# State space products in 64x64 quarters of the array, one per group

## The chip, the cores and the metric

One core of a Trainium2 chip runs the whole kernel. The metric is the device time of one execution in microseconds. TensorE multiplies (a stationary block of up to 128x128 weights is loaded, a moving operand streams past it, results go to PSUM), VectorE and ScalarE do the elementwise work, GpSimd sets constants up, and most transfers are issued from SyncE's queue.

## The reference

A hybrid decoder layer over 16 meta tokens and 256 tokens of width 2048, all in float32:

```
h = RMSNorm(x);  q|k|v|u = h @ W_in
a = sliding-window attention(q, k, v)         16 heads, 4 kv heads, window 128, ALiBi, sinks
s = GLU(S5(u))
x += concat(RMSNorm(a), RMSNorm(s)) @ W_out
x += relu(RMSNorm(x) @ W_up)^2 @ W_down       8192 wide
```

The part that the change touches is S5, a diagonal state space model: 64 groups of 16 channels, each of which drives a complex state of 64 entries.

```
lam_bar = exp(lam * delta);  b_bar = ((lam_bar - 1) / lam) * b
state[t] = lam_bar * state[t-1] + b_bar @ u[t]
y[t] = Re(c @ state[t]) + d * u[t];  g = gelu(y);  s = g * sigmoid(g @ W_glu + b_glu)
```

## The kernel before

Large products split float32 operands into a high and a low part (hi, lo) and take three products of these; weights arrive in units of 512 KB, and `part` has ScalarE write hi and VectorE write lo, up to four units ahead of their use. The phases follow each other on TensorE: u0, k, v, q0, u1, q1, u2, u3 (projections), then wt (the attention half of W_out), g (GLU), wb (the other half of W_out), and the MLP (up, dn). Attention and the state space model are side work, generators that `step` feeds between the units. A planner keeps a clock for VectorE, ScalarE and TensorE, adds a price to it for each instruction (`product` prices TensorE), and feeds side work as long as the two vector clocks run less than `lead` ahead of TensorE's. A scheduler of the language then orders each engine's instructions by a simulation, with priorities. Each engine and SyncE's queue execute in order.

The state space model works in chunks of CT = 4 tokens: 68 chunks (4 of meta tokens, 64 of tokens). Groups are taken in 32 pairs (the pair's two groups fill 128 rows: 2 x 64 states), and the pairs in four sets Q of 8. For each Q:

- `prod` (L621) builds a table of 8 x 4 x 16 entries per state row from the powers of lam_bar (Fr, Fi, Ar, Ai) and b or c: three VectorE operations into a temporary, then two ScalarE copies that spread the two groups into a table of 8 x 4 x 2 x 16, so that each group sits beside zeros.
- `ssm_in` (L639) builds Vr, Vi; `ssm_vt` (L652) transposes them, 16 transposes of 128x128 and four copies from PSUM.
- `ssm_out` (L672) builds Wr, Wn; takes kp, the response of a chunk to itself, with products of 128x32 weights; spreads it with a mask (gm) into the first 32 rows of MT, adds the diagonal d on VectorE, and copies shifted blocks of it to the other rows with three transfers inside SBUF.
- `ssm_states` (L739): z = VT x U, two products of 128x128 by 68 for each pair, then VectorE rotates them; `ssm_scan` (L771) runs the recurrence on VectorE.
- `ssm_y` (L805): y = MT x U + Wr x Xr + Wn x Xi, three products of 128x128 by 64 for each pair; Gelu on ScalarE; a transfer to DRAM (dg) and four back into gT, whose rows are channels.

U is u in rows of (token in the chunk, group, channel); `u_out` (L705) writes it to DRAM and reads it back with four transfers. Every 128x128 block of VT, Wr, Wn and MT is block diagonal over the pair's two groups: half of it is zeros.

```
q = slice(64 * hf, 64 * hf + 64)
nc.tensor.matmul(sp[:, 0:144], lhsT=self.qT[q, m, 0:P], rhs=self.KT[q, j, 0:144], start=True, stop=True)
```

These two lines of `score` (L956) are the one place of before where products of half the rows alternate: heads lie in rows 0-63 and 64-127, and each head writes a PSUM tile of its own.

`late` is a one that ScalarE makes when attention is done; what is scaled with it can't run earlier, so that Gelu's table is loaded once Exp is over.

Of the kernel before, what the change touches and what calls it, by code (L numbers as in the profile page):

```python
# [29 lines left out]
CT = 4  # L30
# [34 lines left out]

class Paced:
# [19 lines left out]
class PacedCore:  # L86
# [8 lines left out]
    def product(self, out, kw):  # L95
        n = math.prod(out.shape[1:])
        return 0.11 * PRICE[2] if "rhs" not in kw else n / 2400 if kw["rhs"].dtype == F32R else PRICE[2] * max(n, math.prod(kw["lhsT"].shape[1:])) / 600
# [5 lines left out]
class Trunk:  # L103
# [232 lines left out]
    def constants(self):  # L336
        nc, c = self.nc, self.cst

        w = self.st.tile([P, D // 2], F32, tag="xn", bufs=4, name="zeros")[:, 0:256]
# [149 lines left out]
    def ssm_params(self):  # L489
# [48 lines left out]
        pw = lambda nm, n: sp.tile([P, n, NPAIR], F32, name=nm)  # L538
# [82 lines left out]
    def prod(self, Q, z, xr, xi, yr, yi, op):  # L621

        tt = self.tt
        js = slice(8 * Q, 8 * Q + 8)
        vb = lambda a: a[:, js, :].unsqueeze(2).to_broadcast([P, 8, CT, 16])
        fb = lambda a: a[:, :, js].rearrange("p s j -> p j s").unsqueeze(3).to_broadcast([P, 8, CT, 16])
        t5 = self.spb.tile([P, 8, CT + 1, 16], F32, tag="gt0", bufs=2, name=f"gt0_{Q}")
        t0, t1 = t5[:, :, 1:, :], self.spb.tile([P, 8, CT, 16], F32, tag="gt1", name=f"gt1_{Q}")
        tt(t0, vb(xr), fb(yr), MULT)
        tt(t1, vb(xi), fb(yi), MULT)  # L630
        yield
        tt(t0, t0, t1, op)
# [4 lines left out]
        return t5  # L637

    def ssm_in(self, Q):  # L639
# [4 lines left out]
        if Q == 0:  # L644
            nc.vector.tensor_reduce(out=self.gm, in_=self.m8.rearrange("p (k x) -> p x k", x=2), axis=AX.X, op=ADD)
            nc.vector.tensor_reduce(out=self.blk2, in_=self.m8.rearrange("p (x k) -> p x k", x=2), axis=AX.X, op=ADD)
        Vr, Vi = self.ops[0:2]
        (br, bi) = self.B
        yield from self.prod(Q, Vr, br, bi, self.Fr, self.Fi, SUB)
        yield from self.prod(Q, Vi, br, bi, self.Fi, self.Fr, ADD)  # L650

    def ssm_vt(self, Q):  # L652
        nc = self.nc
        VT = []
        Vr, Vi = self.ops[0:2]
        for nm, V in (("r", Vr), ("i", Vi)):
            vt = self.spb.tile([P, 8, P], F32, tag=f"VT{nm}", name=f"VT{nm}{Q}")
            v2 = V.rearrange("p j s g h -> p j (s g h)")
            for n0 in (0, 4):
                tp = self.ps(f"!vt{nm}{Q}_{n0}").rearrange("p (n c) -> p n c", c=P)  # L660
                for n in range(4):
                    nc.tensor.transpose(out=tp[:, n, :], in_=v2[:, n0 + n, :], identity=self.ident)
                nc.scalar.activation(vt[:, n0:n0 + 4, :], tp, AF.Copy)
                yield
            VT.append(vt)
# [6 lines left out]
    def ssm_out(self, Q):  # L672
# [4 lines left out]
        Vr, Vi, Wr, Wn = self.ops  # L677
        MT = self.MT
        cr, nci = self.C
        Wc = []  # L680
        for W, c, a in ((Wr, cr, (self.Ar, self.Ai)), (Wn, nci, (self.nAi, self.Ar))):
            t = yield from self.prod(Q, W, cr, nci, *a, ADD)
            nc.scalar.activation(t[:, :, 0, :], c[:, js, :], AF.Copy)
            Wc.append(t)

        kp = self.ps(f"!kp{Q}")[0:32, :].rearrange("p (j h) -> p j h", h=64)
        for n in range(8):
            for k, (V, w) in enumerate(zip((Vr, Vi), Wc)):
                nc.tensor.matmul(kp[:, n, :], lhsT=V[:, n, 3, :, :].rearrange("p g h -> p (g h)"),
                                 rhs=w[:, n, 0:CT, :].rearrange("p k h -> p (k h)"), start=k == 0, stop=k == 1)  # L690
            if n % 4 == 3:
                yield
        q = slice(0, 32)
        for g in range(2):
            nc.scalar.activation(MT[q].rearrange("p j (k g h) -> p (j k) g h", g=2, h=16)[:, :, g, :],
                                 kp.rearrange("p j (k h) -> p (j k) h", h=16), AF.Copy, scale=self.gm[q, g:g + 1])
        dI = self.spb.tile([P, 8, CT, 16], F32, tag="gt1", name=f"dI{Q}").rearrange("p j s h -> p (j s h)")[:, 0:256].rearrange("p (j h) -> p j h", h=32)
        tt(dI[q], self.ident[q, q].unsqueeze(1).to_broadcast([32, 8, 32]), self.dd[q, js].unsqueeze(2).to_broadcast([32, 8, 32]), MULT)
        tt(MT[q, :, 0:32], MT[q, :, 0:32], dI[q], ADD)
        yield  # L700
        for t in range(1, CT):
            nc.sync.dma_start(out=MT[32 * t:32 * t + 32, :, 32 * t:], in_=MT[q, :, 0:P - 32 * t])
        yield

    def u_out(self, mp, acc):  # L705
# [10 lines left out]
        def back():  # L716
            for s in range(CT):
                self.nc.sync.dma_start(out=self.U[32 * s:32 * s + 32, 8 * mp:8 * mp + 8, :].rearrange("r (q m) c -> r q (m c)", q=4),
                                       in_=dr[:, s, :, :].rearrange("(q r) m c -> r q (m c)", q=4))
# [19 lines left out]
    def ssm_states(self, Q):  # L739
# [65 lines left out]
    def ssm_y(self, Q):  # L805
        nc, X, MT, (Wr, Wn) = self.nc, self.X, self.MT, self.ops[2:4]
# [254 lines left out]
    def attn_end(self):  # L1061
# [291 lines left out]
```

## Time and profile before

| what | value |
|---|---|
| median of 3 runs | 1052.19 us (1051.99 to 1052.55) |
| profiled execution, its own time | 1052.78 us |
| its span | 1051.0 us |
| granted TensorE clock | 0.999 |
| TensorE, VectorE, ScalarE busy | 99%, 64%, 49% |
| HBM read, written | 186.03 MB, 4.26 MB |
| state space work lies between | 30 and 275 us of the span |

PE is TensorE, PEld its weight loads, DVE VectorE, ACT ScalarE, POOL GpSimd, SPq SyncE's queue. In a group of instructions stand line, engine, operation, output <- inputs, shapes and count, then busy us and mean ns of one, then idle time of the engine before them and what ended it. A matmul's end is modelled, and ends of neighbours overlap: what one costs is read from the distance of starts, or from the pieces of the chain of waits. The functions of the planner hand instructions on, so most rows carry a helper's line (L80, L81); go by the names of the tiles.

### The profile page before, as it was taken

To read this page: it belongs to the slowest core of one execution; us is meant where nothing else is said; L and a number is where in the kernel's file an instruction comes from. 1 tells how busy PE (TensorE), PEld (TensorE's weight loads), DVE (VectorE), ACT (ScalarE), POOL (GpSimd) and SP (SyncE) were. 2 spreads that over 40 slices of the span, in tenths; PEclk is the share of its full clock that TensorE was granted. 3 is DMA by queue.
4 is the path that set the end of the run, shared out by engine and by line. 5 is a ranking of instruction groups with operands and counts; after the bars stand their busy time and mean duration, and the time that the engine had idled before them with its cause. 6 is when DMAs were issued, how large, how long until landed. Compare 5 with 4: busy or idle time off the path is not lost.

```text
span 1051.0 us, 14959 instructions
## 1 busy us (share of the span) xinstructions
PE 1043.7 (99%) x5732; PEld 897.5 (85%) x5732; DVE 670.5 (64%) x1108; ACT 518.4 (49%) x744; POOL 10.1 (1%) x62
## 2 busy tenths in 40 slices
PE   8999999999999999999999999999999999999998
PEld 7989788888988888888888888888888888888886
DVE  8998877758677766555466655556565545665553
ACT  5845767563656544433445443344453344544332
POOL 3000000000000000000000000000000000000000
PEclk9999999999999999999999999999999999999999
DMA  9663424345556666566666656566656666665763
GB/s 323 219 201 103 141 90 149 104 148 179 166 177 196 184 191 190 186 194 197 193 190 185 196 185 197 193 189 196 187 185 194 198 189 194 184 195 184 216 216 105
DMA packets 145994, 192.07 MB, mean 183 GB/s; under 512 B 9697, under 2 KB 97889, under 8 KB 145537
## 3 DMA queue, kind: packets, MB, share of 16 engines
q1 hardware_dynamic: 145360, 190.54, 58.0%
q8 instruction: 45, 0.74, 0.3%
q10 hardware_dynamic: 560, 0.56, 0.2%
q14 instruction: 29, 0.23, 0.1%
HBM read 186.03 MB, written 4.26 MB: 181 GB/s over the span
## 4 chain that ended last, share of the span: by engine, by line
PE 98%; DMA 1%; ACT 0%; SPq 0%; issue 0%; DVE 0%; ACTq 0%
PE up L81 34%; PE dn L81 33%; PE u L81 5%; PE q L81 4%; PE wt L81 4%; PE wb L81 4%; PE y L80 2%; PE g L81 2%; PE pv L80 2%; PE k L81 1%; PE z L80 1%; PE v L81 1%; PE s L80 1%; PE kp L80 1%; DMA xT<-in_xT 1%; PE pt L80 1%
## 5 line engine op out<-in xcount | busy, mean ns | idle before, releaser
L80 DVE TENSOR_TENSOR lo<-raw,hi 128x1024 fp32r<-128x1024 f32 x328 | 401.1, 1223 | 284.6 <-ACT hi L80 284.2
L80 ACT ACTIVATE hi<-raw 128x1024 fp32r<-128x1024 f32 x328 | 347.3, 1060 | 363.7 <-PE dn L81 195.5
L81 PE MATMUL up<-h,hi 128*128 128x512 f32 x1024 | 245.6, 391 | 0.0
L81 PEld LDWEIGHTS up<-h,hi 128*128 128x128 f32 x1024 | 188.1, 188 | 36.2
L81 PE MATMUL dn<-hi,ah 128*128 128x512 f32 x512 | 199.2, 389 | 0.0
L81 PE MATMUL dn<-lo,ah 128*128 128x512 f32 x512 | 199.2, 389 | 0.0
L81 PE MATMUL dn<-hi,al 128*128 128x512 f32 x512 | 199.2, 389 | 0.0
L81 PEld LDWEIGHTS up<-h,lo 128*128 128x128 f32 x1024 | 131.5, 191 | 5.1
L81 PE MATMUL up<-h,lo 128*128 128x256 f32 x1024 | 133.1, 283 | 0.0
L81 PEld LDWEIGHTS dn<-hi,ah 128*128 128x128 f32 x512 | 96.1, 188 | 20.0
L81 PEld LDWEIGHTS dn<-hi,al 128*128 128x128 f32 x512 | 96.1, 188 | 20.0
L81 PEld LDWEIGHTS dn<-lo,ah 128*128 128x128 f32 x512 | 96.1, 188 | 19.8
L81 ACT ACTIVATE r<-up 128x256 f32<-128x256 f32 x64 | 24.0, 375 | 56.3 <-PE up L81 56.3
L81 DVE TENSOR_TENSOR r<-up,r 128x256 f32<-128x256 f32 x64 | 26.9, 421 | 29.0 <-ACT r L81 29.0
L81 PE MATMUL wt<-hi,ma 128*128 128x512 f32 x128 | 41.0, 399 | 0.0
L81 PE MATMUL u<-hTl,hi 128*128 128x272 f32 x96 | 28.9, 301 | 0.0
L81 PE MATMUL u<-hTh,lo 128*128 128x272 f32 x96 | 28.6, 298 | 0.0
L81 PEld LDWEIGHTS wt<-hi,ma 128*128 128x128 f32 x128 | 23.7, 188 | 5.3
L81 PE MATMUL u<-hTh,hi 128*128 128x272 f32 x96 | 28.3, 295 | 0.0
L81 ACT ACTIVATE ah<-s 128x512 fp32r<-128x512 f32 x32 | 20.2, 632 | 16.0 <-DVE s L81 16.0
L81 DVE SCALAR_TENSOR_TENSOR xm<-dn,rs_h,xm 128x512 f32<-128x512 f32 x32 | 22.5, 743 | 7.8 <-PE dn L81 7.8
L81 PE MATMUL q<-lo,hTh 128*128 128x512 f32 x64 | 25.8, 404 | 0.0
(292 smaller groups left out, 1154.8 us busy)
## 6 DMA issues: line engine op xcount, KB each, us to landing
raw<-in_w_up SPq DMA_DIRECT2D x128, 512.0 KB, 3.9
raw<-in_w_down SPq DMA_DIRECT2D x128, 512.0 KB, 3.8
raw<-in_w_in SPq DMA_DIRECT2D x39, 512.0 KB, 4.3
raw<-in_w_out SPq DMA_DIRECT2D x32, 512.0 KB, 4.1
raw<-in_w_glu SPq DMA_DIRECT2D x8, 512.0 KB, 4.3
x<-in_x SPq DMA_DIRECT2D x4, 512.0 KB, 8.4
xm<-in_x SPq DMA_DIRECT2D x2, 1024.0 KB, 7.7
out<-xm SPq DMA_DIRECT2D x8, 256.0 KB, 5.1
```

The source lines that it names most:

```text
L80: return f(*args, **kw)
L81: return f(*args, **kw)
```

## The change

The two groups of a pair are no longer one 128x128 product with zeros, but two of 64x64: rows and columns 0-63 for one, 64-127 for the other, into the same PSUM tile. The tables lose their zeros, and a row of a table is ordered (channel, token in the chunk). The powers lie as (pair, power). V and W are written by VectorE straight into the tables. V is turned by products with the identity in place of transposes. kp reads a small copy V3, which alone keeps the zeros, and a W shifted by one power, wc. MT is laid out in `km` on 32 partitions, one copy for each token of the chunk, with the diagonal written by ScalarE, and goes through DRAM into 128 rows. U and gT come back in one transfer each. The planner's price of such a product is halved, and the buffers for rows of x are six.

```
-        return ... else PRICE[2] * max(n, math.prod(kw["lhsT"].shape[1:])) / 600
+        return ... else PRICE[2] * max(n, math.prod(kw["lhsT"].shape[1:])) * kw["lhsT"].shape[0] / P / 600
...
-        self.ops = [self.spb.tile([P, 8, CT, 2, 16], F32, name=nm) for nm in ("Vr", "Vi", "Wr", "Wn")]
-        self.MT = self.spb.tile([P, 8, P], F32, name="MT")
-        nc.vector.memset(self.ops[0], 0.0)
-        for z in self.ops[1:] + [self.MT]:
-            g.memset(z, 0.0)
+        self.km = self.spb.tile([P, CT * 513], F32, name="km")[0:32, :]
+        self.V3 = self.spb.tile([P, 2, 8, 2, 16], F32, name="V3")
+        nc.vector.memset(self.km, 0.0)
+        g.memset(self.V3, 0.0)
...
-        t = self.st.tile([P, D // 2], F32, tag="xn", bufs=4, name=f"x{k}{h}")[0:src.shape[0], :]
+        t = self.st.tile([P, D // 2], F32, tag="xn", bufs=6, name=f"x{k}{h}")[0:src.shape[0], :]
...
-        pw = lambda nm, n: sp.tile([P, n, NPAIR], F32, name=nm)
+        pw = lambda nm, n: sp.tile([P, NPAIR, n], F32, name=nm).rearrange("p j s -> p s j")
...
-        vb = lambda a: a[:, js, :].unsqueeze(2).to_broadcast([P, 8, CT, 16])
-        fb = lambda a: a[:, :, js].rearrange("p s j -> p j s").unsqueeze(3).to_broadcast([P, 8, CT, 16])
-        t5 = self.spb.tile([P, 8, CT + 1, 16], F32, tag="gt0", bufs=2, name=f"gt0_{Q}")
-        t0, t1 = t5[:, :, 1:, :], self.spb.tile([P, 8, CT, 16], F32, tag="gt1", name=f"gt1_{Q}")
-        tt(t0, vb(xr), fb(yr), MULT)
+        vb = lambda a: a[:, js, :].unsqueeze(3).to_broadcast([P, 8, 16, CT])
+        fb = lambda a: a[:, :, js].rearrange("p s j -> p j s").unsqueeze(2).to_broadcast([P, 8, 16, CT])
+        t1 = self.spb.tile([P, 8, 16, CT], F32, tag="gt1", name=f"gt1_{Q}")
+        tt(z, vb(xr), fb(yr), MULT)
         tt(t1, vb(xi), fb(yi), MULT)
         yield
-        tt(t0, t0, t1, op)
-        for g in range(2):
-            q = slice(64 * g, 64 * g + 64)
-            self.nc.scalar.activation(z[q, :, :, g, :], t0[q], AF.Copy, scale=1.0 if self.late is None else self.late[q, :])
+        tt(z, z, t1, op)
...
-            for n0 in (0, 4):
-                tp = self.ps(f"!vt{nm}{Q}_{n0}").rearrange("p (n c) -> p n c", c=P)
-                for n in range(4):
-                    nc.tensor.transpose(out=tp[:, n, :], in_=v2[:, n0 + n, :], identity=self.ident)
-                nc.scalar.activation(vt[:, n0:n0 + 4, :], tp, AF.Copy)
+            tp = self.ps(f"!vt{nm}{Q}").rearrange("p (n c) -> p n c", c=64)
+            for n in range(8):
+                for q in GROUPS:
+                    nc.tensor.matmul(tp[q, n, :], lhsT=V[q, n, :, :].rearrange("p h s -> p (h s)"), rhs=self.ident[q, q], start=True, stop=True)
+            nc.scalar.activation(vt, tp, AF.Copy)
...
+            nc.scalar.activation(w[:, :, :, 0], c[:, js, :], AF.Copy)
+            nc.scalar.activation(w[:, :, :, 1:], W[:, :, :, 0:CT - 1], AF.Copy)
...
+        for k, V in enumerate(self.ops):
+            for g, q in enumerate(GROUPS):
+                nc.scalar.activation(self.V3[q, k, :, g, :], V[q, :, :, 3], AF.Copy)
...
-        for t in range(1, CT):
-            nc.sync.dma_start(out=MT[32 * t:32 * t + 32, :, 32 * t:], in_=MT[q, :, 0:P - 32 * t])
+        for s in range(CT - 1):
+            o = one if self.late is None else self.late[0:32, :]
+            nc.scalar.activation(km[:, s, :, :, s + 1:], kp[:, :, :, 1:CT - s], AF.Copy, scale=o)
+        tt(dI, kp[:, :, :, 0], dI, ADD)
+        same = self.km.rearrange("p (s x) -> p s x", x=513)[:, :, 0:512].rearrange("p s (y k) -> p s y k", k=CT)[:, :, :, 0]
+        nc.scalar.activation(same, dI.rearrange("p j h -> p (j h)").unsqueeze(1).to_broadcast([32, CT, 128]), AF.Copy, ...)
+        dk = self.dram.tile([32, CT * 512], F32, name=f"dk{Q}")
+        nc.sync.dma_start(out=dk, in_=self.km[:, 0:CT * 512])
+        self.MT = self.spb.tile([P, 8, 64], F32, tag="MT", name=f"MT{Q}")
+        nc.sync.dma_start(out=self.MT.rearrange("p j x -> p (j x)"), in_=dk.rearrange("r (s x) -> (r s) x", s=CT))
...
-                    nc.tensor.matmul(z[k][:, n, :], lhsT=VT[k][:, 4 * o + n, :], rhs=self.U[:, j0 + 4 * o + n, :], start=True, stop=True)
+                    for q in GROUPS:
+                        nc.tensor.matmul(z[k][q, n, :], lhsT=VT[k][q, 4 * o + n, :], rhs=self.U[q, j0 + 4 * o + n, :], start=True, stop=True)
...
-            nc.tensor.matmul(yp[:, n, :], lhsT=MT[:, n, :], rhs=self.U[:, 8 * Q + n, MCH:NCH], start=True, stop=False)
-            for k, W in enumerate((Wr, Wn)):
-                nc.tensor.matmul(yp[:, n, :], lhsT=W[:, n, :, :, :].rearrange("p s g h -> p (s g h)"), rhs=X[k][:, n, MCH - 1:NCH - 1], start=False, stop=k == 1)
+            for q in GROUPS:
+                nc.tensor.matmul(yp[q, n, :], lhsT=MT[q, n, :], rhs=self.U[q, 8 * Q + n, MCH:NCH], start=True, stop=False)
+            for k, W in enumerate(self.W):
+                for q in GROUPS:
+                    nc.tensor.matmul(yp[q, n, :], lhsT=W[q, n, :, :].rearrange("p h s -> p (h s)"), rhs=X[k][q, n, MCH - 1:NCH - 1], start=False, stop=k == 1)
```

Here `GROUPS = (slice(0, 64), slice(64, 128))`.

More of the change, by code (lines that the diff above doesn't have):

```diff
@@ L63 @@
 FAR = -1e32
+GROUPS = (slice(0, 64), slice(64, 128))
 class Paced:
@@ L96, in product @@
         n = math.prod(out.shape[1:])
-        return 0.11 * PRICE[2] if "rhs" not in kw else n / 2400 if kw["rhs"].dtype == F32R else PRICE[2] * max(n, math.prod(kw["lhsT"].shape[1:])) / 600
+        return 0.11 * PRICE[2] if "rhs" not in kw else n / 2400 if kw["rhs"].dtype == F32R else PRICE[2] * max(n, math.prod(kw["lhsT"].shape[1:])) * kw["lhsT"].shape[0] / P / 600
     def __getattr__(self, name):
@@ L337, in constants @@
         nc, c = self.nc, self.cst
-        w = self.st.tile([P, D // 2], F32, tag="xn", bufs=4, name="zeros")[:, 0:256]
+        w = self.st.tile([P, D // 2], F32, tag="xn", bufs=6, name="zeros")[:, 0:256]
         nc.vector.memset(w, 0.0)
@@ L643, in ssm_in @@
             nc.gpsimd.tensor_scalar(self.C[1], self.C[1], -1.0, None, op0=MULT)
-        if Q == 0:
-            nc.vector.tensor_reduce(out=self.gm, in_=self.m8.rearrange("p (k x) -> p x k", x=2), axis=AX.X, op=ADD)
             nc.vector.tensor_reduce(out=self.blk2, in_=self.m8.rearrange("p (x k) -> p x k", x=2), axis=AX.X, op=ADD)
-        Vr, Vi = self.ops[0:2]
+            self.i16 = self.cst.tile([32, 16], F32, name="i16")
+            self.tt(self.i16, self.ident[0:32, 0:16], self.ident[0:32, 16:32], ADD)
         (br, bi) = self.B
-        yield from self.prod(Q, Vr, br, bi, self.Fr, self.Fi, SUB)
-        yield from self.prod(Q, Vi, br, bi, self.Fi, self.Fr, ADD)
+        self.ops = [self.spb.tile([P, 8, 16, CT], F32, tag=nm, name=f"{nm}{Q}") for nm in ("Vr", "Vi")]
+        yield from self.prod(Q, self.ops[0], br, bi, self.Fr, self.Fi, SUB)
+        yield from self.prod(Q, self.ops[1], br, bi, self.Fi, self.Fr, ADD)
     def ssm_vt(self, Q):
@@ L654, in ssm_vt @@
         VT = []
[L655 to L658, printed above, removed]
-            for n0 in (0, 4):
-                tp = self.ps(f"!vt{nm}{Q}_{n0}").rearrange("p (n c) -> p n c", c=P)
-                for n in range(4):
-                    nc.tensor.transpose(out=tp[:, n, :], in_=v2[:, n0 + n, :], identity=self.ident)
-                nc.scalar.activation(vt[:, n0:n0 + 4, :], tp, AF.Copy)
-                yield
+        for nm, V in zip("ri", self.ops):
+            vt = self.spb.tile([P, 8, 64], F32, tag=f"VT{nm}", name=f"VT{nm}{Q}")
+            tp = self.ps(f"!vt{nm}{Q}").rearrange("p (n c) -> p n c", c=64)
+            for n in range(8):
+                for q in GROUPS:
+                    nc.tensor.matmul(tp[q, n, :], lhsT=V[q, n, :, :].rearrange("p h s -> p (h s)"), rhs=self.ident[q, q], start=True, stop=True)
+                if n == 3:
+                    yield
+            nc.scalar.activation(vt, tp, AF.Copy)
+            yield
             VT.append(vt)
@@ L676, in ssm_out @@
         js = slice(j0, j0 + 8)
-        Vr, Vi, Wr, Wn = self.ops
-        MT = self.MT
+        one = 1.0 if self.late is None else self.late
         cr, nci = self.C
[L680 to L686, printed above, removed]
+        self.W, Wc = [], []
@@ new lines, in ssm_out @@
+        for nm, c, a in (("Wr", cr, (self.Ar, self.Ai)), ("Wn", nci, (self.nAi, self.Ar))):
+            W, w = (self.spb.tile([P, 8, 16, CT], F32, tag=m, name=f"{m}{Q}") for m in (nm, nm + "c"))
+            yield from self.prod(Q, W, cr, nci, *a, ADD)
+            nc.scalar.activation(w[:, :, :, 0], c[:, js, :], AF.Copy)
+            nc.scalar.activation(w[:, :, :, 1:], W[:, :, :, 0:CT - 1], AF.Copy)
+            self.W.append(W)
+            Wc.append(w)
+        for k, V in enumerate(self.ops):
+            for g, q in enumerate(GROUPS):
+                nc.scalar.activation(self.V3[q, k, :, g, :], V[q, :, :, 3], AF.Copy)
@@ L687, in ssm_out @@
+        yield
+        kp = self.ps(f"!kp{Q}")[0:32, :].rearrange("p (j h k) -> p j h k", h=16, k=CT)
         for n in range(8):
-            for k, (V, w) in enumerate(zip((Vr, Vi), Wc)):
-                nc.tensor.matmul(kp[:, n, :], lhsT=V[:, n, 3, :, :].rearrange("p g h -> p (g h)"),
-                                 rhs=w[:, n, 0:CT, :].rearrange("p k h -> p (k h)"), start=k == 0, stop=k == 1)
+            for k, w in enumerate(Wc):
+                nc.tensor.matmul(kp[:, n, :, :].rearrange("p h k -> p (h k)"), lhsT=self.V3[:, k, n, :, :].rearrange("p g h -> p (g h)"),
+                                 rhs=w[:, n, :, :].rearrange("p h k -> p (h k)"), start=k == 0, stop=k == 1)
@@ L691, in ssm_out @@
             if n % 4 == 3:
                 yield
[L693 to L698, printed above, removed]
@@ L699, in ssm_out @@
-        tt(MT[q, :, 0:32], MT[q, :, 0:32], dI[q], ADD)
-        yield
-        for t in range(1, CT):
-            nc.sync.dma_start(out=MT[32 * t:32 * t + 32, :, 32 * t:], in_=MT[q, :, 0:P - 32 * t])
+        dI = self.spb.tile([P, 8, 16], F32, tag="dI", name=f"dI{Q}")[0:32, :, :]
+        tt(dI, self.i16.unsqueeze(1).to_broadcast([32, 8, 16]), self.dd[0:32, js].unsqueeze(2).to_broadcast([32, 8, 16]), MULT)
+        km = self.km[:, 0:CT * 512].rearrange("p (s j h k) -> p s j h k", s=CT, h=16, k=CT)
@@ new lines, in ssm_out @@
+        for s in range(CT - 1):
[3 more added lines that the diff above has]
+        same = self.km.rearrange("p (s x) -> p s x", x=513)[:, :, 0:512].rearrange("p s (y k) -> p s y k", k=CT)[:, :, :, 0]
+        nc.scalar.activation(same, dI.rearrange("p j h -> p (j h)").unsqueeze(1).to_broadcast([32, CT, 128]), AF.Copy, scale=one if self.late is None else self.late[0:32, :])
@@ L703, in ssm_out @@
+        yield
+        dk = self.dram.tile([32, CT * 512], F32, name=f"dk{Q}")
+        nc.sync.dma_start(out=dk, in_=self.km[:, 0:CT * 512])
+        yield
+        self.MT = self.spb.tile([P, 8, 64], F32, tag="MT", name=f"MT{Q}")
+        nc.sync.dma_start(out=self.MT.rearrange("p j x -> p (j x)"), in_=dk.rearrange("r (s x) -> (r s) x", s=CT))
         yield
@@ L716, in back @@
         def back():
-            for s in range(CT):
-                self.nc.sync.dma_start(out=self.U[32 * s:32 * s + 32, 8 * mp:8 * mp + 8, :].rearrange("r (q m) c -> r q (m c)", q=4),
-                                       in_=dr[:, s, :, :].rearrange("(q r) m c -> r q (m c)", q=4))
+            self.nc.sync.dma_start(out=self.U[:, 8 * mp:8 * mp + 8, :].rearrange("r (q m) c -> r q (m c)", q=4),
+                                   in_=dr.rearrange("(q r) s m c -> (r s) q (m c)", q=4))
             self.ready.add(mp)
@@ L805, in ssm_y @@
     def ssm_y(self, Q):
[L806 removed]
+        nc, X, MT = self.nc, self.X, self.MT
         yp = self.ps(f"!y{Q}").rearrange("p (n c) -> p n c", c=XCH)
         for n in range(8):
[L809 to L811 removed]
+            for q in GROUPS:
[3 more added lines that the diff above has]
+                    nc.tensor.matmul(yp[q, n, :], lhsT=W[q, n, :, :].rearrange("p h s -> p (h s)"), rhs=X[k][q, n, MCH - 1:NCH - 1], start=False, stop=k == 1)
             if n % 4 == 3:
@@ L818, in ssm_y @@
         nc.scalar.activation(gs, yp, AF.Gelu_apprx_tanh, scale=one)
-        dr = self.dram.tile([P, 8, XCH], F32, name=f"dg{Q}")
-        nc.sync.dma_start(out=dr, in_=gs)
+        dr = self.dram.tile([4, P, 2, XCH], F32, name=f"dg{Q}")
+        nc.sync.dma_start(out=dr.rearrange("q p m c -> p q (m c)"), in_=gs.rearrange("p (q m) c -> p q (m c)", m=2))
         yield
-        for q in range(4):
-            nc.sync.dma_start(out=self.gT[32 * q:32 * q + 32, :, 2 * Q:2 * Q + 2, :].rearrange("r t m c -> r t (m c)"),
-                              in_=dr[:, 2 * q:2 * q + 2, :].rearrange("(t r) m c -> r t (m c)", t=CT))
+        nc.sync.dma_start(out=self.gT[:, :, 2 * Q:2 * Q + 2, :].rearrange("r t m c -> r t (m c)"),
+                          in_=dr.rearrange("q (r t) m c -> (q r) t (m c)", t=CT))
         yield
```

5 lines of the change are left out of this document (removed).

## The prediction

> **What bounds the kernel now.** I read the page first: busy shares, then the chain that ended last.
>
> ```profile
> span 1051.0 us, 14959 instructions
> PE 1043.7 (99%) x5732; PEld 897.5 (85%) x5732; DVE 670.5 (64%) x1108; ACT 518.4 (49%) x744; POOL 10.1 (1%) x62
> PE 98%; DMA 1%; ACT 0%; SPq 0%; issue 0%; DVE 0%; ACTq 0%
> ```
>
> The chain of waits lies on TensorE for 98% of the span, so any time that TensorE doesn't need is time won, as long as the other engines keep up. The change touches only the state space part, which lies between 30 and 275 us; the MLP behind it is left alone. So I went to the pieces of the chain in order of time, where runs of one product stand without their modelled tails (start, length, what, how many records):
>
> ```profile
> 32.83 0.87 PE vtr L80 x8
> 43.76 1.90 PE kp L80 x32
> 65.76 1.73 PE z L80 x16
> 74.28 0.84 PE z L80 x8
> 97.95 4.86 PE y L80 x44
> 111.46 1.60 PE s L80 x12
> 145.68 0.90 PE kp L80 x14
> 162.50 0.91 PE s L80 x8
> 166.76 0.90 PE s L80 x4
> ```
>
> One fp32 product is two records, one transpose is one. A record with 128 weight columns costs 0.87/8 = 109 ns (vtr), 0.84/8 = 105 ns (z), 4.86/44 = 110 ns (y), though z and y stream only 68 and 64 columns. kp has 32 weight columns and streams 64: 18 more records cost 1.90 - 0.90 = 1.00 us, so 55.6 ns each, and 0.12 us a run is left over. A record is thus paid by the wider of its two sides, and a 64-column one should cost about 55.6 ns. The counts come from the groups by line:
>
> ```profile
> L80 PE MATMUL y<-X,Wn 128*128 128x64 f32 x64 | 12.3, 273 | 0.0
> L80 PE MATMUL z<-U,VTi 128*128 128x68 f32 x64 | 9.8, 273 | 0.0
> L80 PE MATMUL vti<-ident,Vi 128*128 128x128 f32 x32 | 4.8, 273 | 0.0
> ```
>
> y has three such groups (MT, Wr, Wn: 192 records), z two (128), the transposes two (64). At the prices above that is 192 x 110 = 21.1, 128 x 106 = 13.6 and 64 x 109 = 7.0 us: 41.7 us of TensorE in all.
>
> **The change part by part.** *Quarters.* Each 128x128 block is half zeros: two groups on its diagonal. Now each group has a product of its own, 64 rows by 64 columns, in the top left or the bottom right quarter of the array. Records double: y 384, z 256, vt 256 (64 products become 128, and the transpose form, one record, becomes a product with the identity, two). At 55.6 ns, and z at 55.6 x 68/64 = 59 ns, that is 21.3 + 15.1 + 14.2 = 50.7 us if they run one behind the other, half of it, 25.3 us, if two quarters run at once. So the whole gain hangs on the overlap. The nearest rows are those of the attention scores, whose heads lie in rows 0-63 and 64-127 by turns:
>
> ```profile
> L80 PE MATMUL s<-KT,qT x8: 283/388/389, 162.4 to 163.0; 64*128 64x144 f32 x4, 64*128 64x272 f32 x4
> L80 PE MATMUL s<-KT,qT x4: 282/388/389, 117.5 to 118.1; 64*128 64x144 f32 x2, 64*128 64x272 f32 x2
> ```
>
> Two heads (8 records) run from 162.4 to 163.0 us by their starts, one head (4 records) from 117.5 to 118.1; the pieces say the same, 0.91 against 0.90 us. Two row halves do run at once here, wholly. What no row shows is two halves that write one PSUM bank: the two heads have a bank each, the two quarters write partitions 0-63 and 64-127 of the same one. Bounds: no overlap, 50.7 - 41.7 = +9.0 us; full overlap, 25.3 - 41.7 = -16.4 us. I take the full overlap, because the row half is what the s rows have in common with the change and the partitions written are disjoint. Against it stands the Trainium skill, "TensorEngine Tiling (Array Packing)", section Gotcha 1: PSUM Pressure: row tiles can't access one PSUM bank at the same time. No run here shows that yet; by it the first bound would hold, and it is a rival below.
>
> *Switching.* A third head after a pair costs 1.60 - 0.90 = 0.70 us, a lone one 0.90: entering and leaving the 64-row form costs 0.20 us. The weight load after the scores shows where it goes: it can't be drawn ahead.
>
> ```profile
> 118.40 0.30 PEld L80 LDWEIGHTS z<-U,VTi 128*128 128x128 f32 x2 [0.36 <-issue]
> ```
>
> The z runs of before show no such cost (16 records 1.73, 8 records 0.84). Counting the pieces of the chain, vt, z and y stand in 34 separate runs (12, 16 and 6; y starts twice more right behind vt). At 0.20 us that is +6.8 us; bounds 34 x 0.12 (kp) = +4.1 and 34 x 0.36 = +12.2 us. I take 0.20, which is the same kind of switch.
>
> *Tables.* V and W are written by VectorE into the table that the product reads; the two spreading copies on ScalarE per table fall away. kp keeps its 128x32 by 64 form and its 128 records, so it costs the same. ScalarE, VectorE rows that price it:
>
> ```profile
> L81 ACT ACTIVATE Vr<-gt 64x512 f32<-64x512 f32 x8 | 5.0, 624 | 0.1
> L81 ACT ACTIVATE VTr<-vtr 128x512 f32<-128x512 f32 x8 | 4.6, 591 | 3.3 <-PE vtr L80 3.1
> L81 ACT ACTIVATE MT<-kp,gm 32x512 f32<-32x512 f32 x6 | 3.7, 670 | 6.5 <-PE y L80 5.2 <-PE kp L80 1.2
> L81 ACT ACTIVATE gt<-bc 128x128 f32<-128x128 f32 x8 | 2.4, 306 | 0.2
> L81 ACT ACTIVATE sg<-g,vecs 128x256 f32<-128x256 f32 x1 | 0.7, 711 | 0.0
> L81 DVE TENSOR_TENSOR gt<-bc,Fr 128x512 f32<-128x512 f32 x8 | 5.5, 685 | 1.3 <-DMA bc<-in_ssm_bc 0.8 <-PE kp L80 0.5
> L81 DVE TENSOR_TENSOR w<-z,cb 128x272 f32<-128x272 f32 x16 | 7.0, 436 | 3.0 <-PE z L80 2.9
> L81 DVE TENSOR_TENSOR ub<-u,rb 128x272 f32<-128x272 f32 x6 | 3.9, 644 | 0.6 <-PE u L81 0.6
> L81 DVE TENSOR_TENSOR MT<-MT,dI 32x256 f32<-32x256 f32 x4 | 1.6, 412 | 8.9 <-ACT MT L81 8.9
> ```
>
> ScalarE per quarter Q of the groups: removed are 8 spreads x 0.62, 2 MT x 0.67 and 2 VT x 0.59, 7.5 us. Added are 2 shifted copies of W (384 elements, at most 0.62), 4 small V3 copies (0.31), 3 copies of kp (at most 0.67) and the spread diagonal, 512 elements written every fourth word: 0.67 as MT, or 2 x 0.71 = 1.42 as sg, which writes 256 that way. Sum 5.2 to 5.9 us. So ScalarE gains some 2 us per Q; it waits for others anyway, and I count nothing.
>
> VectorE: 12 products of 512 elements per Q stay. Their innermost run falls from 16 to 4, each operand contiguous or constant along it. If that costs nothing they stay at 0.685; if it costs as reading every fourth word does (ub 644 against w 436 for 272 elements, 1.48 times), 48 x 0.33 = +15.8 us of VectorE in the whole kernel. I take nothing, since no operand steps by four. The powers themselves do now lie four words apart where they are computed, in about 30 operations of 32 to 128 elements; (644 - 436)/272 = 0.76 ns an element makes that about +1.5 us in the stretch before the first V, none of it in front of TensorE, which is in the k projection there. The two diagonal operations go from 2 x 0.41 to about 2 x 0.3 us. Zeroing: one memset on each engine instead of one and four, before the first weights land; nothing.
>
> *Transfers.* MT takes a write to DRAM and a read behind it instead of three copies inside SBUF; U and gT come in one transfer instead of four.
>
> ```profile
> U<-du SPq DMA_DIRECT2D x16, 68.0 KB, 2.7
> dg<-gs SPq DMA_DIRECT2D x4, 256.0 KB, 2.1
> gT<-dg SPq DMA_DIRECT2D x16, 64.0 KB, 2.0
> MT<-MT SPq DMA_DIRECT2D x4, 96.0 KB, 2.2
> ```
>
> MT is needed tens of us later, behind the states and the scan, so its two hops (some 2 x 2.2 us) are hidden. The read waits on SP for the write, and behind it stand the weight loads; but weights are split up to four units ahead, a unit being 24 products of 0.125 us, 3 us, so 2 or 3 us are covered. Without that cover it would be 4 x 2.2 = 9 us. Six buffers for the rows of x let the last two loads start earlier; weights of the k projection are by then on their way. Nothing. At the end of the part the path from y to gT loses three issues, about 1 us, and the changed prices in the planner move the side work about; I give that +-3 us.
>
> **Sum.** -16.4 + 6.8 = -9.6 us of TensorE; I give back 0.8 for places where VectorE doesn't follow. The profiled execution took 1052.78 us (span 1051.0 and 1.78 around it), 0.59 above the median of 1052.19. So 1052.78 - 8.8 = 1044.0, and against the median **1043.4 us**. With the bounds of the switch and the 3 us, the likeliest case's own range is 1038 to 1048.
>
> **Does VectorE follow?** Busy time in stretches (us: PE, PEld, DVE, ACT):
>
> ```profile
> 30.00:50.00 20.00, 20.00 (x156) 18.61 (x155) 19.40 (x51) 16.75 (x30) 0.00 (x0) 1.00 0.64 205
> 50.00:70.00 20.00, 20.00 (x117) 16.87 (x117) 20.00 (x45) 10.08 (x15) 0.00 (x0) 1.00 0.60 170
> 70.00:100.00 30.00, 30.00 (x235) 27.96 (x233) 28.41 (x70) 14.73 (x24) 0.12 (x1) 1.00 0.48 143
> 100.00:160.00 60.00, 60.00 (x399) 50.98 (x398) 44.95 (x123) 41.64 (x92) 0.11 (x1) 1.00 0.38 114
> 160.00:216.00 56.00, 56.00 (x432) 49.72 (x432) 42.77 (x117) 32.74 (x86) 0.00 (x0) 1.00 0.42 138
> 216.00:271.00 55.00, 55.00 (x291) 46.11 (x290) 38.35 (x63) 26.34 (x35) 0.00 (x0) 1.00 0.50 156
> ```
>
> Up to 100 us VectorE is as full as TensorE (67.8 of 70); from 100 to 216 us it has 28 us free. What TensorE saves before 100 us (about a quarter) can only be cashed later, but there is room for it.
>
> **The rivals.** (a) *VectorE sets the pace* up to the end of attention: what TensorE saves there turns into waits for VectorE, and only the wt stretch (216 to 271 us, VectorE 70%) gives its share: z of the last Q 32 x 106 - 32 x 59 ns = 1.5 us, y 48 x 110 - 48 x 55.6 ns = 2.6, less five switches, 1.0: -3.1 us, 1049. For it the full rows up to 100 us, and the possible 15.8 us of slower products; against it the 28 free us. (b) *The quarters don't overlap*, for the bank or another reason: +9.0 + 6.8 = +15.8 us, 1068. The mechanism sits in each vt, z and y run. It decides from the point where the overlap won is less than 50.7 + 6.8 - 41.7 = 15.8 of the 25.4 us to be had, 62%. For it: no row of two halves in one bank. Against it: the s rows. (c) *Switches dear, about 0.36 us or more, or more runs than before*: -16.4 + 12.2 and a few us, 1047 to 1054. For it the 0.36 of the weight load.
>
> **Chances.** Forecast 0.50, (a) 0.22, (b) 0.17, (c) 0.11. A measurement here tells 0.2% (2.1 us) from no change. Faster by more: 0.49 of the forecast, 0.17 of (a) and 0.04 of (c), 0.70; within it: 0.01, 0.05 and 0.04, 0.10; slower: 0.17 of (b) and 0.03 of (c), 0.20. The range 1036 to 1058 holds the forecast, (a) and (c) and leaves out (b) and a small tail below.
>
> **What would show it.** Right: the 96 records of y of a Q in about 48 x 55.6 ns + 0.2 = 2.9 us, 16 records of z in 8 x 59 ns + 0.2 = 0.7 us, the two quarters starting pairwise; the first mlp product about 9 us sooner; no idle time on PE before y. Wrong: y still at 96 x 55.6 ns = 5.3 us (b); gaps on PE released by VectorE before z or y, or between attention and wt (a); weight loads idle for issue by over 0.3 us at each run (c); a gt product over 0.8 us; a unit's split waiting for its transfer behind MT's read.

## The result and the profile after

The changed kernel is slower: 1062.18 us median (1060.05 to 1063.76) against 1052.20 of before on the same chip, a ratio of 1.0092 with a 95% interval of 1.0079 to 1.0106. The forecast was 1043.4 us with a range up to 1058. The profiled execution took 1061.41 us (span 1059.7, granted clock 0.992), 8.7 us of span more than before. Of the executions below, one of e1, which took 1284.63 us at a granted clock of 0.751, is left out.

The page of the changed kernel, span, busy shares and shares of the chain:

```profile
span 1059.7 us, 15927 instructions
PE 1048.9 (99%) x6244; PEld 891.0 (84%) x6244; DVE 671.2 (63%) x1108; ACT 509.4 (48%) x735; POOL 6.7 (1%) x59
PE 90%; DVE 5%; DMA 2%; ACT 2%; issue 1%; ACTq 0%; DVEq 0%
```

TensorE's share of the chain fell from 98 to 90%; VectorE, transfers and ScalarE now stand in it. "Busy" still says 99%, which hides what follows. First the pieces of the chain that answer to those of the prediction (start, length, what, records; all views are of the changed kernel where no other is named):

```profile
68.12 6.06 PE q L84 x26
...
75.81 0.62 PE z L83 x16
76.43 0.23 PE vtp L83
76.66 0.62 PE z L83 x16
77.28 4.62 PE q L84 x19
81.89 1.08 PE vtr L83 x32
...
92.62 0.26 PE y L83 x4
92.88 3.95 PE u L84 x30
96.83 2.71 PE y L83 x88
```

The quarters overlap wholly. The 88 records of y take 2.71 us, the 32 of vtr 1.08: 28 pairs more cost 1.63 us, 58 ns a pair, and 0.15 us a run is left over. One after the other the 88 would take 4.9 us. z takes 0.62 us for 16 records (8 x 59 ns plus 0.15). At these prices y, z and the transposes stream 11.1 + 7.6 + 7.4 = 26.1 us in place of 41.7 (estimate): 15.6 us less, where 16.4 were forecast. The rule of the Trainium skill in "TensorEngine Tiling (Array Packing)", section Gotcha 1: PSUM Pressure, by which row tiles can't access one PSUM bank at the same time, is not borne out for quarters on the diagonal: they write partitions 0-63 and 64-127 of one bank, and the 2.71 us leave no room for turns.

Second, what surrounds a run of quarters. Behind y, 30 records of u take 3.95 us, 132 ns each; behind z, 19 of q take 4.62, 243 ns each, where 26 undisturbed ones took 6.06 or 233 ns. In both pieces about 0.2 us stands at the start. The cost of leaving the small form lies in the piece behind it. Before had it too, in three pieces that the prediction did not read (before):

```profile
163.75 3.01 PE u L81 x24
...
168.64 0.90 PE s L80 x4
169.54 2.21 PE u L81 x16
```

24 records of u at 125 ns, and behind a score 16 at 138 ns: 0.20 us more than 16 x 125. I count a change of form wherever two neighbouring records of TensorE use different numbers of rows or columns of the array: 69 in before, 148 in the changed kernel. Third, the end of attention in the changed kernel, where y of Q = 2 is scattered in single products (two records of one quarter, with no partner to overlap):

```profile
210.88 0.25 PE y L83 x2
211.13 0.26 PE at L83
211.39 0.26 PE y L83 x2
211.64 4.85 PE pv L83 x20
216.50 0.40 PE y L83 x2
216.90 0.62 PE at L83 x2
```

The same 20 records of pv took 2.72 us before, and 2.73 in e3 below (before):

```profile
194.90 2.72 PE pv L80 x20
```

The stretches show why (start:end, length, then busy us of PE, PEld, DVE, ACT, POOL, then the granted clock, the share of the DMA engines, GB/s):

```profile
52.00:54.00 2.00, 1.16 (x14) 0.94 (x13) 1.97 (x5) 0.37 (x2) 0.00 (x0) 1.00 0.82 219
54.00:56.00 2.00, 1.07 (x23) 1.07 (x25) 1.76 (x7) 0.00 (x0) 0.00 (x0) 0.81 0.81 206
56.00:58.00 2.00, 2.00 (x20) 1.87 (x17) 0.13 (x1) 0.00 (x0) 0.00 (x0) 0.50 0.99 355
...
210.00:212.00 2.00, 2.00 (x18) 1.48 (x16) 0.00 (x0) 0.00 (x0) 0.00 (x0) 1.00 0.56 212
212.00:214.00 2.00, 2.00 (x9) 1.42 (x8) 0.00 (x0) 0.00 (x0) 0.00 (x0) 0.56 0.55 142
214.00:216.00 2.00, 2.00 (x11) 2.00 (x11) 0.00 (x0) 0.00 (x0) 0.00 (x0) 0.50 0.00 1
...
224.00:226.00 2.00, 2.00 (x6) 1.42 (x5) 2.00 (x7) 0.69 (x2) 0.00 (x0) 0.52 0.03 8
```

TensorE's granted clock falls to one half at 55 and at 212 us. Summed over larger stretches of the same view:

```profile
50.00:60.00 10.00, 8.23 (x82) 7.83 (x81) 7.63 (x23) 1.78 (x4) 0.00 (x0) 0.83 0.74 240
60.00:180.00 120.00, 118.64 (x1082) 99.09 (x1082) 99.67 (x251) 69.14 (x138) 0.23 (x2) 1.00 0.48 142
210.00:230.00 20.00, 20.00 (x94) 15.10 (x93) 8.57 (x20) 6.86 (x17) 0.00 (x0) 0.66 0.12 37
280.00:290.00 10.00, 8.34 (x67) 7.74 (x66) 3.48 (x5) 5.28 (x8) 0.00 (x0) 1.00 0.41 134
```

The clock costs TensorE 10 x 0.17 + 20 x 0.34 = 8.5 us. Before, it stood at 1.00 in every one of these stretches, as in the third of them (before):

```profile
210.00:230.00 20.00, 20.00 (x134) 17.32 (x133) 9.19 (x25) 13.30 (x26) 0.00 (x0) 1.00 0.44 147
```

The first fall follows a wait. x arrives sooner with six buffers, so the scheduler puts the first z inside v, and TensorE stands until u is back from DRAM:

```profile
51.95 2.94 DMA U<-du
54.89 0.04 issue
54.93 1.93 PE z L83 x32
```

At the end of the state space part the chain leaves TensorE for gs's way through DRAM:

```profile
276.92 3.84 DMA dg<-gs
280.76 0.02 issue
280.77 3.07 DMA gT<-dg
```

### The profile page after: what moved, and what is told of

Its sections match the earlier page's. It is cut to its first block, busy times and chain, and to the rows that moved or that the text cites. A ratio compares the mean times of both kernels' runs of the same rounds, so it can differ in the third digit from the quotient of the medians.

```text
span 1059.7 us, 15927 instructions
## 1 busy us (share of the span) xinstructions
PE 1048.9 (99%) x6244; PEld 891.0 (84%) x6244; DVE 671.2 (63%) x1108; ACT 509.4 (48%) x735; POOL 6.7 (1%) x59
## 4 chain that ended last, share of the span: by engine, by line
PE 90%; DVE 5%; DMA 2%; ACT 2%; issue 1%; ACTq 0%; DVEq 0%
PE up L84 34%; PE dn L84 33%; PE wt L84 4%; PE wb L84 4%; PE q L84 4%; PE u L84 2%; PE pv L83 2%; PE y L83 1%; PE g L84 1%; DVE room L84 1%; PE z L83 1%; DVE lo L83 1%; PE s L83 1%; PE pt L83 1%; DMA U<-du 1%
## 5 line engine op out<-in xcount | busy, mean ns | idle before, releaser
L84 PE MATMUL wt<-lo,ma 128*128 128x512 f32 x64 | 26.1, 408 | 0.0
```

What stands on the lines that cost most here:

```text
L84: return f(*args, **kw)
```

## The experiments

**Theory O**: the overlap was won and then lost by order: the planner's and scheduler's new order scatters the quarters, each scattered run pays its switches, and the thin stretches let the clock fall. **Rival V**: VectorE's chain (up to q0, and again in the last Q) and the transfers at the end set the time, so that what TensorE saves becomes waiting. The clock differs between executions of one program, so the table has the fastest execution beside the median; an experiment is compared at equal clock wherever it matters. e1 to e12 were spread over four chips, on each of which before had a median of 1052.3 to 1052.5 us. The ratio compares all executions of a run with those of before on the same chip; where they scatter (e3, e5), it is not the ratio of the medians.

| run | median us | ratio, 95% | fastest at clock | lowest clock, its time |
|---|---|---|---|---|
| after | 1062.18 | 1.0092, 1.0079 to 1.0106 | 1060.05 at 0.993 | 0.990, 1063.76 |
| e1_price | 1054.95 | 1.0027, 1.0010 to 1.0045 | 1052.64 at 0.998 | 0.987, 1062.71 |
| e2_yfirst | 1052.87 | 1.0006, 0.9995 to 1.0018 | 1051.07 at 0.998 | 0.992, 1057.72 |
| e3_xn4 | 1062.99 | 1.0109, 1.0092 to 1.0126 | 1055.22 at 1.000 | 0.987, 1070.01 |
| e4_xn4_yfirst | 1052.99 | 1.0000, 0.9986 to 1.0013 | 1049.36 at 1.000 | 0.994, 1054.78 |
| e5_yfirst_zlate | 1050.75 | 1.0000, 0.9975 to 1.0025 | 1048.38 at 0.999 | 0.986, 1063.14 |
| e6_xn4_yfirst_zlate | 1048.47 | 0.9962, 0.9949 to 0.9975 | 1047.72 at 0.999 | 0.993, 1054.28 |
| e7_full | 1063.74 | 1.0098, 1.0074 to 1.0122 | 1058.20 at 1.000 | 0.992, 1066.05 |
| e8_yserial | 1059.84 | 1.0065, 1.0052 to 1.0078 | 1058.05 at 0.999 | 0.997, 1059.91 |
| e9_order_full | 1055.23 | 1.0027, 1.0016 to 1.0038 | 1055.16 at 1.000 | 0.999, 1055.23 |
| e10_gt4 | 1055.62 | 1.0023, 0.9997 to 1.0049 | 1048.62 at 1.000 | 0.986, 1062.21 |
| e11_before_order | 1053.17 | 1.0007, 0.9999 to 1.0016 | 1052.52 at 1.000 | 0.999, 1053.57 |
| e12_e6_price | 1052.61 | 1.0005, 0.9996 to 1.0013 | 1051.48 at 1.000 | 0.997, 1055.90 |

**e1: the planner's price as before.**

```
-        ... * max(n, math.prod(kw["lhsT"].shape[1:])) * kw["lhsT"].shape[0] / P / 600
+        ... * max(n, math.prod(kw["lhsT"].shape[1:])) / 600
```

> One line undone: the planner prices a quarter product as a full one again. In the instruction order this moves only what stands between the last attention values and the first wt products: the transposes of attention's output stay in one run of 12, where the changed kernel has y of Q = 2 in single pairs between them. Theory O (order: quarter products scattered among full ones cost a switch each, and TensorE's granted clock falls to 0.5 from 212 to 226 us because of it): the stretch from 204 to 222 us shrinks by 4 to 7 us, the clock stays at 1 or falls for less time, 1054 to 1058 us. Theory V (VectorE and ScalarE set the pace, and what TensorE saves turns into waits): the stretch keeps its length, 1060 to 1063 us.

7.2 us of the loss go with this one factor, though it changes no instruction, only when side work is fed. The first stages stand as in the changed kernel (q0 starts at 59.5 us, after 59.6); wt starts at 216.75 us instead of 221.91, because y(2) no longer stands scattered among the transposes of attention's output. That is theory O's mechanism, and rival V has none for it. Most of it acts through the clock: the profiled execution of e1 lost 1.7 us to one fall, that of the changed kernel 8.5 to two; the difference is 6.8 of the 8.8 us between them.

**e2: y drawn ahead**, so that its products stand together.

```
         yp = self.ps(f"!y{Q}").rearrange("p (n c) -> p n c", c=XCH)
+        self.nc.tensor.ahead = self.sooner(1000)
...
             if n % 4 == 3:
                 yield
+                self.nc.tensor.ahead = self.sooner(1000)
```

> Products of y get a higher priority in the scheduler (1000 steps ahead instead of 100), nothing else: each Q's y then stands in one run of 88 records behind at most two early pairs. Theory O: as with the price undone and a little more, since also the runs of 1 to 16 products of y among the transposes of attention go: 1052 to 1057 us, granted clock 0.996 or more. Theory V: 1060 to 1063 us, with waits of TensorE for VectorE or ScalarE in place of the switches.

9.3 us faster than the changed kernel, by order alone. wt starts at 216.63 us. Here too the clock carries the larger part: the profiled execution of e2 lost 3.4 us to it, so that 5.1 of the 8.3 us between the profiled executions are the clock's and 3.2 the order's own.

**e3: four buffers for the rows of x** instead of six, and **e4: that and e2**.

```
-        ... tag="xn", bufs=6, ...
+        ... tag="xn", bufs=4, ...
```

> Buffers for rows of x back to four from six, nothing else. The last two rows then load later, as before, and in the instruction order the first z products go back from within the v projection into the q projection, so that TensorE doesn't stand before them until u has come back from DRAM (1.9 us idle at 53 us, and a clock of 0.83 in that ten us). Theory O: k and v together fall from 38.1 to 33 or 34 us, 1056 to 1059 us in all. Theory V: the work only moves, z waits elsewhere, 1060 to 1064 us.

> Both, four buffers for rows of x and y ahead of other products. Theory O: the gains add, 1047 to 1053 us, and the granted clock is back at 0.998. Theory V: 1058 us or more.

By its median e3 gained nothing, and there my expectation missed. k and v do take 32.3 us instead of 38.1. But the work moved, as rival V has it: z still waits 0.7 us at 59 us, and 1.4 instead of 0.5 at 174 to 176 us, so that TensorE is idle for 5.9 us up to 290 us, against 6.4 in the changed kernel. Nor does e3 win at equal clock: it takes 1055.2 us at 1.000, the profiled execution of the changed kernel less its 8.5 us of clock 1052.9 (estimate), with 156 changes of form against 148. And executions of this one program reach from 1055.22 us at clock 1.000 to 1070.01 at 0.987: the scatter of y(2) is still there, and in most executions the clock falls. The profiled one kept full clock through the scatter, and so shows the price of a switch undisturbed:

```profile
212.09 2.73 PE pv L83 x20
214.82 0.26 PE y L83 x2
215.07 0.37 PE at L83 x2
215.44 0.25 PE y L83 x2
215.70 0.26 PE at L83
215.96 0.26 PE y L83 x2
```

Each of these pieces of y is one product of one quarter: its two records start 107 ns apart in the trace, where two quarters start 6 to 7 ns apart. It streams 2 x 55.6 = 111 ns and stands 0.26 us; one transpose streams 109 ns and stands 0.26, two stand 0.37. So entering costs 0.15 us, leaving 0.15, the run of a lone product 0.30. A whole run of quarters costs 0.15 in its own piece and 0.20 in the piece behind it (y and u above; 0.15 and 0.19 for z and q): 0.35 us, or 0.175 a change of form.

e4 is the same as before in its median; where the clock held (three of ten executions), it took 1049.4 us, against 1051.1 of e2 at 0.998, which is some 1049 at full clock (estimate). So beside e2 the buffers are worth nothing at equal clock. Nor do four of them keep the clock: in the profiled execution of e4 it fell at 60 us, where z waits 1.1 us, and again at 179.

**e5: e2, and z put back** in the order, so that it does not stand where its operand is late; **e6: that with four buffers.**

```
             for n in range(4):
+                self.nc.tensor.ahead = lambda: self.tc.high_priority(offset=-100)
```

> On top of y ahead of other products, the products of z get a priority 100 steps below the others, so that in the instruction order they stand behind products that are ready instead of in front of them while u is still on its way through DRAM. Theory O (order and clock): the two idle times of TensorE before z, 1.9 us at 53 us and 0.8 us at 175 us, go, the granted clock stays at 0.998 or more, 1046 to 1051 us. Theory V (VectorE and ScalarE set the pace): what waited before z waits later, behind the scan; 1052 to 1056 us.

> The same with four buffers for rows of x. Theory O: within 2 us of the run with six, 1046 to 1051 us, since the buffers only mattered through the place of the first z. Theory V: 1052 us or more.

q0 now starts at 54.5 us (e5) and 53.9 us (e6), and wt at 212.1 and 212.8. e6 beat both kernels, 1048.47 us. What is left of rival V shows in e5's stage g, 27.3 us against 23.2 before: the stage begins 6.4 us sooner than before, the last y only 2.7, and TensorE stands for 2.7 us until dg and gT have landed. (Up to 1.7 us of the stage are a fall of the clock, at 271 us.) The profiled execution of e6 was the longest of its six, 1054.28 us, and its stretches name the place: z, pv and scores alternate from 179 to 183 us.

```profile
183.00:184.00 1.00, 1.00 (x7) 0.60 (x6) 1.00 (x6) 0.28 (x2) 0.00 (x0) 1.00 1.00 385
184.00:185.00 1.00, 1.00 (x8) 1.00 (x8) 1.00 (x1) 0.00 (x0) 0.00 (x0) 0.77 1.02 328
...
180.00:210.00 30.00, 30.00 (x236) 22.83 (x235) 19.56 (x59) 14.36 (x47) 0.00 (x0) 0.77 0.35 125
```

30 x 0.23 = 6.9 us are lost there to the clock. The four executions at 0.999 and 1.000 took 1047.7 to 1048.6, some 6 us less than this one.

**e7: e2 with y and z as 128x128 products** of neighbouring table entries; the values are not the reference's.

```
-            for q in GROUPS:
-                nc.tensor.matmul(yp[q, n, :], lhsT=MT[q, n, :], rhs=self.U[q, 8 * Q + n, MCH:NCH], start=True, stop=False)
+            c = slice(64 * min(n, 6), 64 * min(n, 6) + P)
+            nc.tensor.matmul(yp[:, n, :], lhsT=MT.rearrange("p j x -> p (j x)")[:, c], rhs=self.U[:, 8 * Q + n, MCH:NCH], start=True, stop=False)
...
```

> y ahead of other products, and y and z as products of 128 weight columns and 128 rows again, with the neighbouring table entries in place of the zeros (what they multiply is not the model's, so y is not the reference's; counts and shapes are those of the kernel before). Only the quarters are taken away, everything else of the change stays. Theory O: streams of y and z cost 16.5 us more, some 22 runs of them need no switch (-4.4 us) and the clock falls less (-2 us): 1060 to 1064 us against 1052.9 with quarters. Theory V: TensorE's time is not what counts before wt, so 1053 to 1056 us.

```profile
95.60 4.86 PE y L83 x44
```

y is back at 4.86 us for 44 records. Medians say 10.9 us more than e2; fastest against fastest, with e2 moved from 0.998 to full clock by 2 us, it is some 9 us of the 16 that y and z save in streaming. The switches explain the rest: e2 has 135 changes of form, e7 94, and 41 x 0.175 = 7.2 us.

**e8: e2 with y's quarters one after the other**, four pairs of one quarter, then four of the other.

```
-        for n in range(8):
-            for q in GROUPS:
+        for h, q, i in ((h, q, i) for h in range(2) for q in GROUPS for i in range(4)):
+            n = 4 * h + i
...
```

> y ahead of other products, and within y four pairs of one quarter first and then the four of the other, where quarters took turns. If the overlap comes from two neighbouring products that lie in different quarters, y of a Q takes twice as long, 5.0 to 5.3 us for 96 records in place of 2.7, and the whole kernel 8 to 11 us more (1061 to 1064) by theory O, 0 to 3 more by theory V. If the array takes products of different quarters out of order, y keeps its 2.7 us.

```profile
95.25 4.97 PE y L83 x92
```

Neighbouring products in the same quarter don't overlap: 92 records in 4.97 us, 54 ns each, where alternating ones take 31. The kernel is 7.0 us slower than e2, a little less than the 8 to 11 expected, for about 4 x 2.2 us of streaming.

**e9: e6's order with y and z as 128x128** (values not the reference's, as in e7), **e10: e6 with the old transfers at the end**, and **e11: the kernel before with the two edits of order.** e10's edit:

```
-        dr = self.dram.tile([4, P, 2, XCH], F32, name=f"dg{Q}")
+        dr = self.dram.tile([P, 8, XCH], F32, name=f"dg{Q}")
-        nc.sync.dma_start(out=dr.rearrange("q p m c -> p q (m c)"), in_=gs.rearrange("p (q m) c -> p q (m c)", m=2))
+        nc.sync.dma_start(out=dr, in_=gs)
...
+        for q in range(4):
+            nc.sync.dma_start(out=self.gT[32 * q:32 * q + 32, ...], in_=dr[:, 2 * q:2 * q + 2, :]...)
```

> The order of e6 (four buffers, y first, z late), but y and z as 128x128 products of neighbouring table entries, so that the output is not the reference's; only V's transposes keep their quarters. What do the quarters of y and z give in the best order? They save 16.5 us of streaming and cost some 22 switches x 0.20 = 4.4 us. Theory O (order and clock ate the gain): in this order they give 16.5 - 4.4 = 12 us, so 1060. Rival V (VectorE's chain up to q and the end chain set the time, and the streaming is hidden): 3 to 5 us, so 1052 to 1054. e7 against e2 gave 8.4 us at equal clock.

> e6 with the old form of gs's way out and back: one write in rows of 8 products, read back in four transfers. In the changed kernel the write takes 3.84 us and the read 3.07 us where before took 6.1 us from gs to the gate with four reads. If the last path sets the end of the part, the write is 1.0 us sooner and the four issues later cost about as much: 1047.5 to 1048.5 (theory: no more than 1 us either way). If the write's 512-byte pieces cost the whole 0.9 us: 1047.6. The forecast's step (three issues saved, 1 us): 1049.5.

> The kernel before with the two edits of order alone (y first, z late; it has four buffers already). Is e6's gain the order's or the quarters'? If the order alone is worth something without the quarters, 1047 to 1050. If the order only mends what the change had broken, nothing: 1051.5 to 1053, and e6 beats it by its quarters. In the kernel before y stands in whole runs already, so theory O says nothing, 1052 +-1.

e9 lies between the two expectations, nearer to rival V's: 1055.2 us, and no execution was under a clock of 0.999. Against e6 at full clock (1047.7 to 1048.6) y's and z's quarters are worth about 7 us. The switches explain why it is not 12: e6 has 131 changes of form, e9 83. 48 x 0.175 us = 8.4, and 16 - 8.4 = 7.6.

e11 gains nothing, 1053.17, so e6's gain is not the order's: the order only lets the quarters' gain through.

e10 has e6's order on TensorE, yet a median 7 us above it, because seven of its twelve executions ran at 0.993 or less. At 0.999 and 1.000 the medians are 1049.25 (three) and 1048.2 (four). So one transfer in place of four is worth about 1.0 us, the forecast's step (few executions, on two chips). Its chain:

```profile
271.53 4.61 DMA dg<-gs
...
276.15 0.56 SPq L838
...
278.04 2.35 DMA gT<-dg
```

Between the two stand three issues of transfers, 1.9 us; from the start of dg to the end of gT it is 8.9 us here and 6.9 in e6, whose write dg takes 3.7 us. e10 also warns about e6: its order is not free of the clock's fall either, and six executions (of which four kept full clock) are few.

**e12: e6 with the planner's price as before** (e1's edit).

> e6 with the planner's price of a product undone as in e1. Does the price still matter once y's priority and z's are set by hand? In the build's order z now stands in 20 runs (16 in e6) and the scores in 15 (13), 36 blocks of quarters against 34. Theory O with the price as one of the causes of the scatter: the priorities have taken over its work, and what is left is 2 blocks and some more mode changes, so +0.2 to +1.5 us, 1048 to 1050 at full clock. If the halved price itself still cost time, 1044 to 1046. How often the clock falls is the second reading: e6's and e10's fall at 183 us stood among z, pv and scores, which are spread otherwise here.

A miss: 1051.5 us at full clock, 3.8 more than e6, where 0.2 to 1.5 were expected, or a gain. Eight more changes of form (139) are 1.4 us of it, and TensorE is idle for 4.9 us up to 290 us where e6 has 3.4, 1.5 us more; the rest stays open. The price that hurt in the changed kernel helps once y and z are placed by hand: what it does is move the order, for the better or the worse.

## Why the prediction was wrong, step by step

| span, profiled executions | forecast | measured |
|---|---|---|
| streaming of y, z, transposes | -16.4 | -15.6 |
| switches | 34 x 0.20 = +6.8 | 79 more changes x 0.175 = +13.8 |
| TensorE without work | +0.8 | +3.2 |
| granted clock | not considered | +8.5 |
| sum | -8.8 | +9.9 (span: +8.7) |

The idle time is the not-busy part of TensorE up to 290 us, 6.4 us after and 3.2 before; pricing all changes of form by the quarters' 0.175 is an estimate. The other kernels bear these prices out. Take the span of a profiled execution, less the clock (half the length of each fall), the changes of form and the idle time:

| kernel | span | clock | changes | idle | rest |
|---|---|---|---|---|---|
| before | 1051.0 | 0.0 | 69 | 3.2 | 1035.7 |
| e9 (y, z as 128x128) | 1055.1 | 0.0 | 83 | 5.1 | 1035.5 |
| after | 1059.7 | 8.5 | 148 | 6.4 | 1018.9 |
| e3 | 1053.5 | 0.0 | 156 | 5.9 | 1020.3 |
| e6 | 1052.6 | 6.8 | 131 | 3.4 | 1019.4 |
| e8 (quarters one after the other) | 1056.3 | 0.0 | 136 | 3.8 | 1028.7 |

The four kernels with y and z as 128x128 (these two, e7 and e11) leave 1035.0 to 1036.0 us, the nine with alternating quarters 1017.7 to 1020.8, and e8 lies above them by about its 4 x 2.2 us. So the streaming that the quarters save is there in each of them, some 16 us, and what differs between them is switches, waits and clock.

- *Overlap, "I take the full overlap": right*, by the rows of y and z and by e8. Rival (b) fell. kp kept 220 ns, as assumed.
- *"34 x 0.20": mis-sized, the first error.* The 0.20 us read from scores was the entering; the leaving lay in the piece behind, which the prediction did not open. A run costs 0.35 us, near the upper bound of 0.36: 34 x 0.35 = 11.9. The other 1.9 us are more changes than 34 runs make, 79 in all. With 13.8 in place of 6.8 the sum would have given about 1050.4, the case that rival (c) described.
- *"Six buffers ... Nothing" and "the changed prices in the planner move the side work about; I give that +-3 us": the second error.* The price alone is 7.2 us by medians (e1), most of it through the clock; the buffers bring the first z before its operand, 1.8 us of waiting and the first fall of the clock, though taking them back alone moves the waits elsewhere (e3). An edit that moves the order has no price of its own until its order is looked at.
- *The clock* was in no part of the forecast, since before showed 0.999. Without its 8.5 us the median would be about 1053.7 (estimate), inside the range and inside rival (c)'s; with them the result lies past the range. e3's executions differ by 14.8 us with nothing else changed.
- *VectorE and ScalarE: "I give back 0.8 for places where VectorE doesn't follow" was too little.* The chain of the changed kernel lies on them and on U's transfers up to 55 us, from 112 to 122 and from 149 to 176 us, and TensorE stands at the end of each, for 1.8, 0.9 and 0.5 us. The prices of their instructions were near. Groups of the changed kernel (busy us, mean ns):

```profile
L84 DVE TENSOR_TENSOR gt<-bc,Fr 128x512 f32<-128x512 f32 x4 | 2.7, 686 | 0.0
L84 ACT ACTIVATE km<-dI 32x512 f32<-32x512 f32 x3 | 3.4, 1123 | 0.1
L84 ACT ACTIVATE V<-Vr 64x128 f32<-64x128 f32 x8 | 3.4, 426 | 0.0
```

  The products kept their 0.69 us with an inner run of 4. Of ScalarE's terms the spread diagonal was right in its upper bound (1.12 against 0.67 to 1.42), the V3 copies cost 0.43 instead of 0.31. ScalarE's busy time fell by 9 us, nothing followed from it. Rival (a) is right in these waits and in the last Q (e5's stage g), a few us; it does not set the time.
- *Transfers: right*, about 1.0 us (e10); MT's two hops released nothing in the chain.

## What to carry to other kernels

Price a switch of the array's form by both ends: the piece that enters it and the first piece of the other kind behind it, and multiply by the runs of the order that will be built, not of the old one. Where a change makes TensorE's pieces smaller, look at the order first (whole runs, no operand that arrives late) and at the granted clock of the stretches where small pieces alternate. An order that gives the gain once can still lose it to the clock in the next execution, so compare executions at equal clock.

## What the hardware showed that was not expected

**The clock falls while TensorE is busy.** At 55 us it fell behind a wait of 1.8 us. At 212 us (after) and 184 us (e6) PE was busy all the time by the trace; but priced by the distances of starts inside undisturbed runs (55.6 ns for a lone record of a quarter, 109 a transpose, 112 for pv), TensorE streamed 0.5 to 0.9 of each of the eight microseconds before the first and 0.6 to 0.8 of the five before the second (estimate). It is not a fixed bound: e3's profiled execution kept 1.00 through the same scatter, at 0.5 to 1.0, and other executions of it did not. The falls have steps: in the kept profiles, what lies behind the last product aside, they last 3.41 us (after, e1, e2, e5, e10) or 2, 4 and 5 times that (6.83 in e4, 13.65 in after and e6, 17.07 in e10), and between the two of the changed kernel lie 45 x 3.41 us. Whether it is the place of these steps that differs between executions of one program is open; no run tried it by itself.

The Trainium skill, "TensorE: Matmul & The Clock Gate", Part 1, has the half rate after an idle window of about 3.4 us; the 0.50 and the 3.41 us agree, but an idle window does not appear at 212 and 184 us. Its section "A second HAM failure mode: psum-queue depth-cycling" tells of a clock that oscillates over frequent small gaps between groups of products; the low streamed shares fit that, but the trace has no gap at either place, and there the clock fell once for four steps and did not swing to and fro.

**A thousandth of mean clock is one microsecond here**: 13.6 us between 1.000 and 0.986 in e10, 14.8 us between 1.000 and 0.987 in e3. One fall costs 1.7 us (at 55) to 6.8 us (at 212) in the profile of the changed kernel.

**Two quarters of the array on its diagonal run at once into one bank** (2.71 us), if they alternate; the same quarter twice in a row does not (4.97).
